# An mLSTM and S5 block: head beginnings, entry of the last head and merge in another order

## The chip, the cores and the metric

The kernel runs on one core of a Trainium2 chip. The metric is the device time of one execution in microseconds (us); lower is better. A core has TensorE (PE, matmuls), VectorE (DVE), ScalarE (ACT), GpSimd (POOL), each with a queue of instructions of its own that it works off in order, and SyncE (SP), whose queue here issues all DMA transfers between DRAM and the on-chip memory. Engines wait for each other through semaphores.

## The reference, cut to what matters

A decoder block over a sequence of 1024 tokens, 1024 channels wide, in float32. Everything is computed from xn, the normalised input:

```python
proj = xn @ w_in[l]
u_a, z_a, o_a, i_a, f_a, u_b, z_b, g_pre = jnp.split(proj, split_points, axis=-1)
y_a = mlstm_branch(u_a, z_a, o_a, i_a, f_a, conv_w[l], conv_b[l], w_q[l], w_k[l], w_v[l],
                   b_i[l], b_f[l], head_g[l], skip_a[l]) @ w_a_out[l]
y_b = s5_branch(...) @ w_b_out[l]
g = jax.nn.sigmoid(g_pre.astype(jnp.float32)).astype(h.dtype)
merged = g[..., :D_MODEL] * y_a + g[..., D_MODEL:] * y_b
h = h + rmsnorm(merged @ w_o[l], norm_post_g[l])
```

The mLSTM branch: c = silu(causal convolution of u_a over 4 tokens), q and k from c, v from u_a, in 4 heads of 256 channels; per head a chunkwise linear attention over 8 chunks of 128 tokens with a running 256 x 256 state; the result times sigmoid(o), normalised per head, times head_g, plus skip times c, times silu(z_a). The S5 branch is done before the stretch that this document is about.

## The kernel before, in words

Every operand of a matmul is split into a high and a low part (suffixes h and l, as xh and xl, wh and wl), and every product is three matmuls: high by high, low by high, high by low, lines 180 to 182. The high part is written by ScalarE (`Copy` into a rounded type), the low part by VectorE or GpSimd (value minus high part). Weights come in as wr and become wh (line 140) and wl (line 142); `take` and `pump` split the next weights ahead of their use.

The order of all instructions is that of the code; nothing reorders them. Work that is not attention is cut into units: a projection of one block of 128 or 256 columns, 24 matmuls of 256 columns or 512 (18 for a y_a unit, which leaves out two of the eight k). They stand in a deque, `fillers`; `fill()` runs the next one, and so the code of a head puts units between the steps of its attention. `run` also does three things around a unit: `tick` issues the stores that wait in `pending`, the loads of the next units are issued (`look` of them ahead), and `step2` runs operations that an earlier unit put off with `defer`.

A head h has for each chunk c: `attn_a(h, c)` (scores of q and k, line 1084, transposes of k, line 1096, and the splits sTh/sTl, ksh/ksl and q2h/q2l by ScalarE and VectorE) and `attn_b(h, c)` (the state and the output, three matmuls each on those splits; VectorE then makes hr). attn_a runs one chunk ahead of attn_b. After chunks 3 and 7 `attn_c` scales hr (line 1170), `attn_d(h, hf)` transposes it (line 1180), adds skip times c and multiplies by silu(z) (lines 1182 and 439), and `attn_e` splits the result and stores it to yh_d and yl_d in DRAM. For the last head the split goes straight into the tiles of k = 6 and 7.

During head h the fillers are the o, u and z units of head h + 1 and `k1`, the second half of k of head h itself. `late` are five units of the next head, run after the last chunk: us[2], ks[0], vs[0], us[3], vs[1] (u for tokens 512 on, two blocks of 128 channels; k and v). A u unit puts off `u_act` and `u_out` (the convolution's silu, its split into hlh and hll, lines 970 to 981, and the store of skip times c to cs_d, line 983). k_unit ends with line 1057, where GpSimd makes q for a half of the sequence, in a single buffer.

In the last head the fillers are the y_a units, (i, half, m): the projection by w_a_out, k = 0 to 5 only. Its input comes back from yh_d and yl_d into the tiles xh and xl, k by k and half by half (`ystep(n)` issues n of these pairs). Each unit loads y_t and y_gb (t1_d and gb_d: gate and S5 part), computes (1 + y_t) times its sum plus a quarter of y_gb (lines 1237, 1238), and stores that to pa_d.

After the heads comes the merge: the last four y_a units (i = 3) are mixed with 16 `mg_unit`s, which add k = 6 and 7 to a block of y_a (weights ya3, their own 2 x 1024 columns), load the stored part (fpa) and the gate (ft), and split the sum into mh and ml. `wo_unit(i, t)`, 32 of them, are the output projection; the fourth of a token block ends with `finish`.

Two pools of PSUM banks hold the sums: `pp` with three banks (units) and `pm` with five (attention).

Of the kernel before, what the change touches and what calls it, by code (L numbers as in the profile page):

```python
# [21 lines left out]
H = 4  # L22
# [14 lines left out]
def hybrid_block(ctx, tc, x, norm_pre_g, w_in, conv_w, conv_b, w_q, w_k, w_v, b_i, b_f, head_g,  # L37
# [1179 lines left out]

    yaux = {}

    def ya_pre(ct, hf, pool=None):  # L1220
        rs = slice(ct * P, (ct + 1) * P)
        pool, a, b, n = (hp, "hlh", "hll", 5) if pool is None else (pool, "ft", "fpa", 7)
        t1 = pool.tile([P, 512], F32, tag=a, bufs=n, name="y_t1")
        SY.dma_start(t1, t1_d[rs, HS[hf]])
        gb = pool.tile([P, 512], F32, tag=b, bufs=n, name="y_gb")
        SY.dma_start(gb, gb_d[rs, HS[hf]])
        yaux[ct, hf] = (t1, gb)

    def ya_unit(i, m, hf):
        if m == 0 and hf == 0 and i < 3:  # L1230
            cur["ya"] = take(("ya", i), i > 0)
        ct = 2 * i + m
        rs = slice(ct * P, (ct + 1) * P)
        t1, gb = yaux.pop((ct, hf))
        o = bank()
        proj_cm(o, cur["ya"], m * P, yh, yl, HS[hf], ks=list(range(6)))
        V.scalar_tensor_tensor(t1, t1, 1.0, o, op0=ALU.add, op1=ALU.mult)
        V.scalar_tensor_tensor(gb, gb, 0.25, t1, op0=ALU.mult, op1=ALU.add)
        store(pa_d[rs, HS[hf]], gb)
# [29 lines left out]
    for h in range(H):  # L1269
# [19 lines left out]
        if h == H - 1:  # L1289
            for i in range(2):  # L1290
                fillers[i][0]()
                fillers[i] = (None,) + fillers[i][1:]
        ystep(4)
        if h < H - 1:
            fill()
        attn_a(h, 0)
        for c in range(NCH):
            if c == 1 or c == 6:
                load_cz(h, c // 4)
            if c == 6 and h == H - 2:  # L1300
# [33 lines left out]
    flush2()
# [6 lines left out]
    mh, ml = {}, {}  # L1341
    maux = {}

    def mg_pre(ct, hf):
        rs = slice(ct * P, (ct + 1) * P)
        t1 = fp.tile([P, 512], F32, tag="ft", bufs=7, name="ft")
        SY.dma_start(t1, t1_d[rs, HS[hf]])
        pr = fp.tile([P, 512], F32, tag="fpa", bufs=7, name="fpa")
        SY.dma_start(pr, pa_d[rs, HS[hf]])
        maux[ct, hf] = (t1, pr)  # L1350

    def mg_unit(ct, hf):
        if ct == 0 and hf == 0:
# [11 lines left out]
    ob, xres = {}, {}  # L1365
    sso = fp.tile([P, NCH, 4], F32, name="sso")

    def wo_unit(i, t):
# [13 lines left out]
        jk = fp.tile([P, 256], F32, tag="fjk", bufs=2, name="fjk")  # L1382
        A.activation(jk, o[:, :256], AF.Square, accum_out=sso[:, t, i:i + 1])
# [15 lines left out]
    def mgf(ct, hf):  # L1399
        fillers.append(unit(lambda: mg_unit(ct, hf), lambda: mg_pre(ct, hf)))  # L1400
# [56 lines left out]
```

## Time and profile before

| what | value |
|---|---|
| median of 3 runs | 1003.8 us (1002.75, 1003.8, 1004.91) |
| profiled execution | 1006.37 us, of which the span in the profile is 1004.3 us |
| TensorE busy | 976.7 us |
| VectorE, ScalarE, GpSimd busy | 615.5, 351.1, 154.6 us |
| mean granted TensorE clock | 0.993 of full speed |

The profile is of one execution. Times in it are microseconds from the span's start; a matmul's end is modelled, since matmuls overlap in the pipe. In a timeline a bracket at a row's end tells how long the engine was idle before it and which instruction (engine, tile, line) ended that; rows of one kind that follow each other are joined (x2). SPq is SyncE's queue.

### The profile page before, as it was taken

To read this page: it belongs to the slowest core of one execution; us is meant where nothing else is said; L and a number is where in the kernel's file an instruction comes from. 1 tells how busy PE (TensorE), PEld (TensorE's weight loads), DVE (VectorE), ACT (ScalarE), POOL (GpSimd) and SP (SyncE) were. 2 spreads that over 40 slices of the span, in tenths; PEclk is the share of its full clock that TensorE was granted. 3 is DMA by queue.
4 is the path that set the end of the run, shared out by engine and by line. 5 is a ranking of instruction groups with operands and counts; after the bars stand their busy time and mean duration, and the time that the engine had idled before them with its cause. 6 is when DMAs were issued, how large, how long until landed. Compare 5 with 4: busy or idle time off the path is not lost.

```text
span 1004.3 us, 15220 instructions
## 1 busy us (share of the span) xinstructions
PE 976.7 (97%) x5617; PEld 840.9 (84%) x5617; DVE 615.5 (61%) x1400; ACT 351.1 (35%) x696; POOL 154.6 (15%) x210
## 2 busy tenths in 40 slices
PE   7999999999999999999999999999999999999997
PEld 6888888788778788978988899889987888779997
DVE  4426496686952854254677477747774888675226
ACT  7322131233032531223544355435543452223311
POOL 4001000000000000012112232223221311343001
PEclk8999999999999999999999999999999999999999
DMA  7344221333056447314433354336436796783504
GB/s 253 94 153 157 90 95 36 93 111 109 17 177 187 170 156 253 107 42 126 138 121 131 95 174 131 135 86 184 132 121 215 248 318 202 271 301 118 189 1 168
DMA packets 115449, 148.31 MB, mean 148 GB/s; under 512 B 19080, under 2 KB 71472, under 8 KB 115376
## 3 DMA queue, kind: packets, MB, share of 16 engines
q1 hardware_dynamic: 115376, 147.35, 45.7%
q8 instruction: 44, 0.72, 0.3%
q14 instruction: 29, 0.24, 0.1%
HBM read 100.88 MB, written 46.43 MB: 147 GB/s over the span
## 4 chain that ended last, share of the span: by engine, by line
PE 83%; DVE 10%; DMA 3%; issue 2%; ACT 1%; SPq 0%; POOL 0%; DVEq 0%; POOLq 0%; ACTq 0%
PE pp L180 22%; PE pp L182 22%; PE pp L181 22%; PE pm L182 4%; PE pm L180 4%; PE pm L181 3%; DVE wl L142 1%; PE pm L1084 1%; DMA wr<-in_w_in_dram 1%; DVE zt L439 1%; PE pm L1007 1%; DMA xt<-in_x_dram 1%; DMA ft<-t_d 1%; PE pm L661 1%; DVE ec_r L439 1%
## 5 line engine op out<-in xcount | busy, mean ns | idle before, releaser
L180 PE MATMUL pp<-xh,wh 128*128 128x512 f32 x768 | 307.6, 401 | 3.2 <-DVE xl L276 2.4
L182 PE MATMUL pp<-xh,wl 128*128 128x512 f32 x768 | 305.0, 397 | 4.4 <-DVE wl L142 4.4
L181 PE MATMUL pp<-xl,wh 128*128 128x512 f32 x768 | 304.7, 397 | 0.0
L182 PEld LDWEIGHTS pp<-xh,wl 128*128 128x128 f32 x768 | 145.0, 189 | 41.0 <-DVE wl L142 6.2
L180 PEld LDWEIGHTS pp<-xh,wh 128*128 128x128 f32 x768 | 145.0, 189 | 39.3 <-DVE xl L276 2.7
L181 PEld LDWEIGHTS pp<-xl,wh 128*128 128x128 f32 x768 | 145.1, 189 | 32.7
L142 DVE TENSOR_TENSOR wl<-wr,wh 128x1024 fp32r<-128x1024 f32 (+2 forms) x71 | 83.4, 1211 | 46.3 <-ACT wh L140 41.7
L140 ACT ACTIVATE wh<-wr 128x1024 fp32r<-128x1024 f32 (+2 forms) x76 | 73.2, 1008 | 40.8 <-PE pm L181 30.7
L182 PE MATMUL pp<-wh,ml 128*128 128x256 f32 x256 | 72.8, 284 | 0.5 <-POOL ml L1363 0.5
L180 PE MATMUL pp<-wh,mh 128*128 128x256 f32 x256 | 72.9, 285 | 0.0
L180 PE MATMUL pp<-wh,xh 128*128 128x256 f32 (+1 forms) x256 | 72.0, 281 | 0.0
L181 PE MATMUL pp<-wl,mh 128*128 128x256 f32 x256 | 71.9, 281 | 0.0
L288 ACT ACTIVATE tg<-pp 128x512 f32<-128x512 f32 x32 | 19.1, 599 | 151.1 <-PE pp L182 75.2
L181 PE MATMUL pp<-wl,xh 128*128 128x256 f32 (+1 forms) x256 | 71.8, 280 | 0.0
L182 PE MATMUL pp<-wh,xl 128*128 128x256 f32 (+1 forms) x256 | 71.8, 280 | 0.0
L182 PEld LDWEIGHTS pp<-wh,ml 128*128 128x128 f32 x256 | 48.1, 188 | 0.7 <-POOL ml L1363 0.7
L181 PEld LDWEIGHTS pp<-wl,mh 128*128 128x128 f32 x256 | 48.6, 190 | 0.1
L180 PEld LDWEIGHTS pp<-wh,mh 128*128 128x128 f32 x256 | 48.4, 189 | 0.2 <-ACT mh L1362 0.2
L181 PEld LDWEIGHTS pp<-wl,xh 128*128 128x128 f32 x256 | 48.2, 188 | 0.2
L180 PEld LDWEIGHTS pp<-wh,xh 128*128 128x128 f32 x256 | 48.1, 188 | 0.2
L182 PEld LDWEIGHTS pp<-wh,xl 128*128 128x128 f32 x256 | 48.0, 187 | 0.0
L981 POOL TENSOR_TENSOR hll<-t2k,hlh 128x512 fp32r<-128x512 f32 x16 | 20.8, 1297 | 166.2 <-ACT hlh L980 89.4
(395 smaller groups left out, 1731.5 us busy)
## 6 DMA issues: line engine op xcount, KB each, us to landing
wr<-in_w_in_dram SPq DMA_DIRECT2D x48, 512.0 KB
t_d<-tg SPq DMA_DIRECT2D x32, 256.0 KB
xt<-in_x_dram SPq DMA_DIRECT2D x8, 512.0 KB
aux<-t_d SPq DMA_DIRECT2D x16, 256.0 KB
gb_d<-aux SPq DMA_DIRECT2D x16, 256.0 KB
so_d<-sow SPq DMA_DIRECT2D x32, 128.0 KB
sz_d<-t2k SPq DMA_DIRECT2D x16, 256.0 KB
cs_d<-t2k SPq DMA_DIRECT2D x16, 256.0 KB
```

What stands on the lines that cost most here:

```text
L140: A.activation(hi, raw, AF.Copy)
L142: eng.tensor_tensor(wl[:, k0:k0 + n, c0:c0 + w], raw, hi.bitcast(F32), op=ALU.subtract)
L180: PE.matmul(o, lh, rh, start=first, stop=False)
L181: PE.matmul(o, lh, rl, start=False, stop=False)
L182: PE.matmul(o, ll, rh, start=False, stop=last)
L288: A.activation(t, o, AF.Tanh, scale=0.5)
L439: V.tensor_tensor(o, a, b, op=op)
L661: PE.matmul(o[NS * b2:NS * (b2 + 1), g * P:(g + 1) * P], q["wt"][:, ri, g, NS * b2:NS * (b2 + 1)], ut[b][:, 2 * g + b2, :], start=True, st ...
L981: PL.tensor_tensor(lo, acc, hi.bitcast(F32), op=ALU.subtract)
L1007: PE.matmul(pm[:, 256 * k:256 * k + 256], wt[:, e, 256 + P * k:256 + P * k + P], wt[:, e, 0:256], start=e == 0, stop=e == 1)
L1084: PE.matmul(sc[:, :P], k_[:, m, sl], q_[:, m, sl], start=m == 0, stop=m == 1)
```

## The change

Five things change. One: at the beginning of each head two fillers run before attn_a(1) and attn_b(0), where one did; one filler fewer follows. Two: at the entry of the last head attn_d(2, 1) comes after us[3], not before it; what is put off is flushed (`flush2`, `tick`) before the head starts; `ystep(2)` issues two pairs of loads there, not four; and in the last head the fillers stand in other places, so that the first y_a unit of the second half (the third unit of the head) runs behind attn_b(0), and k1 before attn_a(3). Three: in the merge the last four y_a units leave their sum in the PSUM bank, and the mg units of the same blocks add k = 6 and 7 to it; these come first in each half; the second half of the weights ya3 is split by GpSimd. Four: wo units are mixed with two fillers each, not three. Five: at the end the sum of three of the four squares is made early, and GpSimd adds the fourth.

```diff
@@ ya_unit
-        proj_cm(o, cur["ya"], m * P, yh, yl, HS[hf], ks=list(range(6)))
+        proj_cm(o, cur["ya"], m * P, yh, yl, HS[hf], ks=list(range(6)), last=i < 3)
+        if i == 3:
+            maux[ct, hf] = (t1, gb, o)
+            return
@@ heads
-        ystep(4)
+        ystep(4 if h < H - 1 else 2)
...
-            fill()
+            fill(2 if c == 0 else 1)
             ystep(3)
...
-            if c % 4 != 3 if h < H - 1 else c in (2, 4, 6):
+            if c in ((1, 2, 4, 5, 6) if h < H - 1 else (4, 6)):
                 fill()
...
-            if i == (3 if h < H - 2 else 2):
+            if i == 3:
                 attn_d(h, 1)
...
+        if h == H - 2:
+            flush2()
+            tick()
...
-    cur["ya"] = take(("ya", 3))
+    cur["ya"] = take(("ya", 3), False)
+    pump(pl=True)
@@ mg_unit
-        t1, pr = maux.pop((ct, hf))
-        o = bank()
-        proj_cm(o, cur["ya3"], ct * P, yh, yl, HS[hf], ks=[6, 7])
+        t1, pr, o = maux.pop((ct, hf))
+        part = o
+        o = bank() if part is None else part
+        proj_cm(o, cur["ya3"], ct * P, yh, yl, HS[hf], ks=[6, 7], first=part is None)
         V.scalar_tensor_tensor(t1, t1, 1.0, o, op0=ALU.add, op1=ALU.mult)
-        tt(t1, t1, pr, ALU.add)
+        if part is None:
+            tt(t1, t1, pr, ALU.add)
+        else:
+            V.scalar_tensor_tensor(t1, pr, 0.25, t1, op0=ALU.mult, op1=ALU.add)
@@ wo_unit
+        if i == 2:
+            V.tensor_reduce(sso[:, t, 4:5], sso[:, t, 0:3], axis=mybir.AxisListType.X, op=ALU.add)
+            V.tensor_scalar(sso[:, t, 4:5], sso[:, t, 4:5], 4.0 * EPS, None, op0=ALU.add)
         if i == 3:
             s = fp.tile([P, 1], F32, tag="fs", bufs=4, name="fs")
-            V.tensor_reduce(s, sso[:, t, :], axis=mybir.AxisListType.X, op=ALU.add)
-            V.tensor_scalar(s, s, 1.0 / D, 4.0 * EPS, op0=ALU.mult, op1=ALU.add)
+            PL.tensor_tensor(s, sso[:, t, 3:4], sso[:, t, 4:5], op=ALU.add)
@@ merge
-    todo = deque((ct, hf) for hf in range(2) for ct in range(KT))
-    for m, hf in ((0, 0), (1, 0), (0, 1), (1, 1)):
-        yaf(m, hf)
-        mgf(*todo.popleft())
-        mgf(*todo.popleft())
-    for ct, hf in todo:
+    yaf(0, 0)
+    yaf(1, 0)
+    for ct in (6, 7, 0, 1, 2, 3):
+        mgf(ct, 0)
+    yaf(0, 1)
+    yaf(1, 1)
+    n_ya = len(fillers)
+    for ct, hf in ((6, 1), (7, 1), (4, 0), (5, 0), (0, 1), (1, 1)):
         mgf(ct, hf)
+    n_hf = len(fillers) - n_ya
+    for ct in range(2, 6):
+        mgf(ct, 1)
...
-        fill(3)
-        if t == 1:
+        fill(2)
+        if t == 2:
             pump()
```

What it moves. First SyncE's queue at the entry of the last head. xh_98 to xh_101 and xl_106 to xl_109 are k = 2 to 5 of the second half, read back; y_t and y_gb belong to a y_a unit. Before, from the last store of head 2:

```order
L82 DMA yl_d<-t2k 128x512
L1066 DMA so<-so_d 128x256 x2
L1224 DMA y_t_7735<-t_d 128x512
L1226 DMA y_gb<-gb_d 128x512
L1215 DMA xh_98<-yh_d 128x512
L1216 DMA xl_106<-yl_d 128x512
L1215 DMA xh_99<-yh_d 128x512
L1216 DMA xl_107<-yl_d 128x512
L1215 DMA xh_100<-yh_d 128x512
L1216 DMA xl_108<-yl_d 128x512
L1215 DMA xh_101<-yh_d 128x512
L1216 DMA xl_109<-yl_d 128x512
```

And in the changed kernel, from the row behind that same store on (xh_101 and xl_109 follow):

```order
L82 DMA cs_d<-t2k 128x512
L1066 DMA so<-so_d 128x256 x2
L1224 DMA y_t_7744<-t_d 128x512
L1226 DMA y_gb<-gb_d 128x512
L1215 DMA xh_98<-yh_d 128x512
L1216 DMA xl_106<-yl_d 128x512
L1215 DMA xh_99<-yh_d 128x512
L1216 DMA xl_107<-yl_d 128x512
L1224 DMA y_t_7768<-t_d 128x512
L1226 DMA y_gb<-gb_d 128x512
L82 DMA pa_d<-y_gb 128x512
L1215 DMA xh_100<-yh_d 128x512
```

The cs_d store has come ahead of all these loads (it stood 20 rows further on), and another y_t, y_gb and a pa_d store ahead of the last four.

Second VectorE in the last head, where the second k unit brings the split of the next weights (L142); sT and q are the products of the next attn_a. Before:

```order
L439 TENSOR_TENSOR ctl<-ct,cth 128x516
L439 TENSOR_TENSOR dec<-dec,msk 128x512
L1237 SCALAR_TENSOR_TENSOR y_t_7763<-y_t_7763,pp 128x512
L1238 SCALAR_TENSOR_TENSOR y_gb<-y_gb,y_t_7763 128x512
L439 TENSOR_TENSOR sT<-pm,dec 128x128
L439 TENSOR_TENSOR q_7970<-q,int 128x256
```

And in the changed kernel, from the same row on:

```order
L439 TENSOR_TENSOR ctl<-ct,cth 128x516
L439 TENSOR_TENSOR dec<-dec,msk 128x512
L142 TENSOR_TENSOR wl<-wr,wh 128x1024
L142 TENSOR_TENSOR wl<-wr,wh 128x512
L439 TENSOR_TENSOR sT<-pm,dec 128x128
L439 TENSOR_TENSOR q_8001<-q,int 128x256
```

The split of the weights stood behind these products and now stands ahead of them; both rows are in the chunk of attn_a(3).

Third VectorE where the merge begins, behind attn_d of the last head. ft and y_t become the merged value, 8598 and 8602 are blocks 6 and 7. Before:

```order
L142 TENSOR_TENSOR wl<-wr,wh 128x1024 x2
L1237 SCALAR_TENSOR_TENSOR y_t_8598<-y_t_8598,pp 128x512
L1238 SCALAR_TENSOR_TENSOR y_gb<-y_gb,y_t_8598 128x512
L1358 SCALAR_TENSOR_TENSOR ft<-ft,pp 128x512
L439 TENSOR_TENSOR ft<-ft,fpa 128x512
```

And in the changed kernel:

```order
L142 TENSOR_TENSOR wl<-wr,wh 128x1024
L1365 SCALAR_TENSOR_TENSOR y_t_8598<-y_t_8598,pp 128x512
L1369 SCALAR_TENSOR_TENSOR y_t_8598<-y_gb,y_t_8598 128x512
L1365 SCALAR_TENSOR_TENSOR y_t_8602<-y_t_8602,pp 128x512
L1369 SCALAR_TENSOR_TENSOR y_t_8602<-y_gb,y_t_8602 128x512
```

One of the two pieces of the split has gone from VectorE (to GpSimd), and blocks 6 and 7 are finished first, without a stored part.

## Rows read from the trace of the kernel before

**Rows 1.** The page, part 1: busy us (share of the span) xinstructions of each engine
```profile
PE 976.7 (97%) x5617; PEld 840.9 (84%) x5617; DVE 615.5 (61%) x1400; ACT 351.1 (35%) x696; POOL 154.6 (15%) x210
```

**Rows 2.** Timeline of TensorE (PE): head beginnings; start, us, line, [idle before <-releaser]
```profile
485.14 0.36 PE L180 MATMUL pm<-vh,ksh 128*128 128x258 f32 x1 [0.66 <-issue]
...
587.67 0.39 PE L180 MATMUL pm<-vh,ksh 128*128 128x258 f32 x1 [0.74 <-ACT ksh L1098]
...
588.50 0.39 PE L182 MATMUL pm<-vh,ksl 128*128 128x258 f32 x1 [0.32 <-DVE ksl L1103]
```

**Rows 3.** Timeline of TensorE: entry of the last head
```profile
777.62 1.46 PE L1180 MATMUL pm<-ident,hr 128*128 128x128 f32 x8 [1.47 <-DVE hr L1170]
...
785.43 0.39 PE L180 MATMUL pm<-wh,hlh 128*128 128x256 f32 x1 [0.40 <-ACT hlh L948]
...
786.16 0.38 PE L182 MATMUL pm<-wh,hll 128*128 128x256 f32 x1 [0.22 <-DVE hll L439]
...
788.50 0.61 PE L1084 MATMUL pm<-q,k 128*128 128x128 f32 x4
...
799.30 0.60 PE L1084 MATMUL pm<-q,k 128*128 128x128 f32 x4
...
801.76 0.40 PE L180 MATMUL pp<-xh,wh 128*128 128x512 f32 x1
...
805.95 0.60 PE L1084 MATMUL pm<-q,k 128*128 128x128 f32 x4
```

**Rows 4.** Timeline of TensorE: the merge
```profile
867.26 0.50 PE L182 MATMUL pp<-xh,wl 128*128 128x512 f32 x1 [0.99 <-DVE wl L142]
...
869.49 0.50 PE L182 MATMUL pp<-xh,wl 128*128 128x512 f32 x1 [1.27 <-DVE wl L142]
...
898.90 0.39 PE L182 MATMUL pp<-wh,ml 128*128 128x256 f32 x1 [0.49 <-POOL ml L1363]
...
902.87 0.50 PE L180 MATMUL pp<-xh,wh 128*128 128x512 f32 x1 [0.56 <-DVE ob L439]
```

**Rows 5.** Timeline of SyncE (SPq): DMA issues at the entry of the last head
```profile
792.78 1.37 SPq L1066 DMA_DIRECT2D so<-so_d  x2
...
799.58 0.46 SPq L1216 DMA_DIRECT2D xl<-yl_d  x1
...
805.37 0.32 SPq L1066 DMA_DIRECT2D so<-so_d  x1
```

**Rows 6.** Timeline of VectorE (DVE): entry of the last head
```profile
785.41 0.69 DVE L439 TENSOR_TENSOR hll<-pp,hlh 128x512 fp32r<-128x512 f32 x1 [1.25 <-ACT hlh L948]
...
795.13 0.69 DVE L971 SCALAR_TENSOR_TENSOR t2k<-t2k 128x512 f32<-128x512 f32 x1
...
811.94 0.42 DVE L1149 SCALAR_TENSOR_TENSOR hr<-so,pm 128x256 f32<-128x256 f32 x1 [0.76 <-DMA so<-so_d]
...
813.36 1.83 DVE L142 TENSOR_TENSOR wl<-wr,wh 128x1024 fp32r<-128x1024 f32 x2 [0.40 <-ACT wh L140]
```

**Rows 7.** Timeline of GpSimd (POOL): entry of the last head, and the end
```profile
798.90 1.29 POOL L981 TENSOR_TENSOR hll<-t2k,hlh 128x512 fp32r<-128x512 f32 x1 [7.54 <-ACT hlh L980]
...
800.16 0.71 POOL L983 TENSOR_SCALAR t2k<-t2k,par 128x512 f32<-128x512 f32 x1
...
808.24 2.78 POOL L1057 TENSOR_TENSOR q<-hlh,hll 128x512 f32<-128x512 f32 x2 [7.38 <-DVE q L439]
...
999.39 0.54 POOL L1389 TENSOR_TENSOR fs<-fs,halfm 128x1 f32<-128x1 f32 x1 [2.34 <-DVE fs L1388]
```

**Rows 8.** Timeline of ScalarE (ACT): second key unit of the last head, and the end
```profile
812.27 1.58 ACT L140 ACTIVATE wh<-wr 128x1024 fp32r<-128x1024 f32 x2
...
998.06 0.38 ACT L1383 ACTIVATE fjk<-pp 128x256 f32<-128x256 f32 x1 [2.40 <-PE pp L182]
```

**Rows 9.** Windows: busy time of each engine, granted TensorE clock, DMA share, GB/s
```profile
300.00:305.00 5.00, 4.27 (x22) 4.11 (x22) 2.52 (x4) 0.00 (x0) 0.00 (x0) 0.66 0.28 106
...
796.00:806.00 10.00, 10.00 (x55) 8.48 (x54) 9.11 (x25) 4.79 (x13) 1.97 (x2) 1.00 0.97 334
```

More of the change, by code (lines that the diff above doesn't have):

```diff
@@ L1216, in ystep @@
             SY.dma_start(yl[k][:, HS[hf]].bitcast(F32), yl_d[k * P:(k + 1) * P, HS[hf]])
-    yaux = {}
+    yaux, maux = {}, {}
     def ya_pre(ct, hf, pool=None):
         rs = slice(ct * P, (ct + 1) * P)
-        pool, a, b, n = (hp, "hlh", "hll", 5) if pool is None else (pool, "ft", "fpa", 7)
+        pool, a, b, n = (hp, "hlh", "hll", 5) if pool is None else (pool, "fyt", "fyg", 2)
         t1 = pool.tile([P, 512], F32, tag=a, bufs=n, name="y_t1")
@@ L1341, in hybrid_block @@
     mh, ml = {}, {}
-    maux = {}
     def mg_pre(ct, hf):
         rs = slice(ct * P, (ct + 1) * P)
-        t1 = fp.tile([P, 512], F32, tag="ft", bufs=7, name="ft")
+        t1 = fp.tile([P, 512], F32, tag="ft", bufs=6, name="ft")
         SY.dma_start(t1, t1_d[rs, HS[hf]])
-        pr = fp.tile([P, 512], F32, tag="fpa", bufs=7, name="fpa")
+        pr = fp.tile([P, 512], F32, tag="fpa", bufs=4, name="fpa")
         SY.dma_start(pr, pa_d[rs, HS[hf]])
-        maux[ct, hf] = (t1, pr)
+        maux[ct, hf] = (t1, pr, None)
     def mg_unit(ct, hf):
-        if ct == 0 and hf == 0:
+        if "ya3" not in cur:
             cur["ya3"] = take("ya3", False)
-        t1, pr = maux.pop((ct, hf))
-        o = bank()
-        proj_cm(o, cur["ya3"], ct * P, yh, yl, HS[hf], ks=[6, 7])
+        t1, pr, o = maux.pop((ct, hf))
+        part = o
+        o = bank() if part is None else part
+        proj_cm(o, cur["ya3"], ct * P, yh, yl, HS[hf], ks=[6, 7], first=part is None)
         V.scalar_tensor_tensor(t1, t1, 1.0, o, op0=ALU.add, op1=ALU.mult)
-        tt(t1, t1, pr, ALU.add)
+        if part is None:
+            tt(t1, t1, pr, ALU.add)
+        else:
+            V.scalar_tensor_tensor(t1, pr, 0.25, t1, op0=ALU.mult, op1=ALU.add)
         mh[ct, hf] = fp.tile([P, 512], F32R, name=f"mh{ct}{hf}")
@@ L1365, in hybrid_block @@
     ob, xres = {}, {}
-    sso = fp.tile([P, NCH, 4], F32, name="sso")
+    sso = fp.tile([P, NCH, 5], F32, name="sso")
     def wo_unit(i, t):
@@ L1382, in wo_unit @@
         jk = fp.tile([P, 256], F32, tag="fjk", bufs=2, name="fjk")
-        A.activation(jk, o[:, :256], AF.Square, accum_out=sso[:, t, i:i + 1])
+        A.activation(jk, o[:, :256], AF.Square, scale=1.0 / 32.0, accum_out=sso[:, t, i:i + 1])
         mul(ob[t][:, cs], o[:, :256], gpo[:, cs])
+        if i == 2:
+            V.tensor_reduce(sso[:, t, 4:5], sso[:, t, 0:3], axis=mybir.AxisListType.X, op=ALU.add)
+            V.tensor_scalar(sso[:, t, 4:5], sso[:, t, 4:5], 4.0 * EPS, None, op0=ALU.add)
         if i == 3:
             s = fp.tile([P, 1], F32, tag="fs", bufs=4, name="fs")
-            V.tensor_reduce(s, sso[:, t, :], axis=mybir.AxisListType.X, op=ALU.add)
-            V.tensor_scalar(s, s, 1.0 / D, 4.0 * EPS, op0=ALU.mult, op1=ALU.add)
+            PL.tensor_tensor(s, sso[:, t, 3:4], sso[:, t, 4:5], op=ALU.add)
             PL.tensor_tensor(s, s, halfm[:, 0:1], op=ALU.pow)
@@ L1399, in mgf @@
     def mgf(ct, hf):
-        fillers.append(unit(lambda: mg_unit(ct, hf), lambda: mg_pre(ct, hf)))
+        fillers.append(unit(lambda: mg_unit(ct, hf), lambda: (ct, hf) in maux or ct > 5 or mg_pre(ct, hf)))
     def yaf(m, hf):
         fillers.append(unit(lambda: ya_unit(3, m, hf), lambda: ya_pre(6 + m, hf, fp)))
-    todo = deque((ct, hf) for hf in range(2) for ct in range(KT))
-    for m, hf in ((0, 0), (1, 0), (0, 1), (1, 1)):
-        yaf(m, hf)
-        mgf(*todo.popleft())
-        mgf(*todo.popleft())
-    for ct, hf in todo:
+    yaf(0, 0)
[6 more added lines that the diff above has]
+    for ct, hf in ((6, 1), (7, 1), (4, 0), (5, 0), (0, 1), (1, 1)):
         mgf(ct, hf)
+    n_hf = len(fillers) - n_ya
+    for ct in range(2, 6):
+        mgf(ct, 1)
     look[0] = 3
@@ L1415, in hybrid_block @@
         fillers[i] = (None,) + fillers[i][1:]
-    fill(10)
+    fill(n_ya)
     pump()
-    fill(4)
+    fill(n_hf)
     for t in range(NCH):
         run(unit(lambda: wo_unit(0, t)))
-        fill(3)
-        if t == 1:
+        fill(2)
+        if t == 2:
             pump()
```

## The prediction

> **What bounds the kernel now.** First the page's busy times: TensorE works 97% of the span [rows 1], so the kernel is bound by its matmuls, and only what TensorE loses by waiting can be gained without taking matmuls away. The change takes none away. Second, therefore, the timeline of TensorE at the places that the diff touches, read by the brackets: idle time before a matmul, and who released it. They show three groups of waits. At the beginning of heads 0, 1 and 2 attn_b(0) waits for the splits of attn_a [rows 2]: 0.66 us in head 0, 0.74 and 0.32 in head 1, and the same pair once more in head 2, so 2.78 us in five waits. At the entry of the last head it waits 1.47 us for hr and 0.40 and 0.22 us for the split u of the last v unit, 2.09 us in three waits [rows 3]. In the merge it waits 0.99 and 1.27 us for the low part of the last y_a weights, 0.49 for ml and 0.56 for a bank that VectorE's ob still holds, 3.31 us in four waits [rows 4]. A wait costs somewhat more than its bracket, since the pipe fills again: the matmul after one shows 0.50 us [rows 4] where an undisturbed one of that shape shows 0.40 [rows 3], and the next starts late as well. I charge 0.15 us for each. Third, the queue of SyncE, because the last head reads its operands back from DRAM while TensorE uses them, and all DMAs stand in that one queue: loads are issued 0.6 us apart there [rows 5], and the 16 DMA engines are 97% busy at 334 GB/s from 796 to 806 us, while TensorE is busy without a gap [rows 9]. That cover is complete, but with nothing to spare.
>
> **The change part by part.**
>
> Head beginnings. With two projection units ahead of attn_a(1), two of 24 short matmuls lie between attn_a(0) and attn_b(0) where one lay, nearly 3 us more in which ScalarE and VectorE make sTh, ksh and ksl. What was missing is under 1.4 us a head, so all five waits are covered: 2.78 + 5 x 0.15 = 3.5 us. Against it stands the tanh of the added o unit, which now stands in ScalarE's queue ahead of attn_a(1)'s operations and writes one of two sow buffers, whose stores were issued late. I leave 0.5 us for that in all three heads (no row shows such a wait; between 0 and 1.5, since the matmuls behind it need these operations only one unit later). Term: -3.0 (-3.5 to -2.0).
>
> Entry of the last head, what goes. attn_d(2,1) comes after the unit us3, 24 long matmuls later, so hr is long scaled when its transposes come; and the transposes stand between us3 and the v unit, which gives the split of u another 1.2 us. 2.09 + 3 x 0.15 = 2.5 us, of which I leave 0.1. Term: -2.4.
>
> Entry of the last head, what comes. The deferred operations of us3 are now flushed before the head starts. They end in a store of c·skip (cs_d) by SyncE, and this store stands ahead of so, of y_t and y_gb and of the loads xh, xl 2 to 5 of the second half; before, it stood behind all of them. With ystep(2) in place of 4, a further pair y_t, y_gb and a pa_d store are also ahead of the last four loads. At the same time the first y_a unit that reads this second half comes earlier: it ran after attn_b(1), and now after attn_b(0).
>
> When can the store be issued? It needs GpSimd's L983, behind L981, behind ScalarE's hlh and VectorE's L971. Before, L971 came 9.7 us after the unit's hll, from 785.41 to 795.13 [rows 6], and the operations between are as long in the new order (four of attn_d, some 2.8 us, take the place of sT, ksl and one y_t, y_gb pair). The unit's hll itself comes 1.62 us of wait and some 1.2 us of transposes (1.46 in their row, with the pipe's end) earlier, at 782.6. So L971 ends at 782.6 + 9.7 + 0.7 = 793.0, hlh 0.6 later, L981 takes 1.29 and L983 0.71 [rows 7]: the store issues at 795.6 in the clock of the old trace. SyncE then needs for the twelve loads what it needed from 792.78 to 799.58, 6.8 us [rows 5], and for the store and three more entries 4 x 0.65: the last xl is issued at 805.0, where it was issued at 799.58.
>
> When has it landed? In bytes, 15 times 256 KB (the two so count as one), 3.93 MB, stand from the store to that load; at 334 GB/s [rows 9] they take 11.8 us, to 807.4, with no delay at either end. From the other side, the so load issued at 805.37 [rows 5] released VectorE at 811.94 [rows 6], 6.6 us later in a full queue: 805.0 + 6.6 = 811.6. I take the middle, 809.5.
>
> When is it wanted? attn_a(0) starts at 788.50 less 2.4, at 786.1. From there to attn_a(2) TensorE took 10.8 us and for attn_a(2) with attn_b(1) 2.46 us, and the unit 4.2 us [rows 3]. The unit now follows after the same 10.8, from 796.9 to 801.1. With the last load at 809.5 and two matmuls behind it, it ends at 810.0. Term: +8.9 (+6.4 to +11.0; less if the DMA engines move these loads faster than the row's mean).
>
> The k unit. It runs before attn_a(3), where it ran after it, and it carries the split of the next y_a weights with it: VectorE's wl, 1.83 us, which waits for ScalarE's wh, 1.58 us [rows 6, 8], stands ahead of the products sT and q2 of attn_a(3). The two GpSimd operations that make q for the second half wait for that q2 (one buffer) and take 2.78 us [rows 7]. From the end Z of the delayed unit: VectorE, busy with its backlog, is through dec at about Z + 6.2; ScalarE's exponentials, k copies and wh, then wl, end at Z + 11.3; q2 at Z + 11.9; q at Z + 14.6. TensorE reaches attn_a(4) after two pairs of attn_a and attn_b (2 x 2.46), the k unit (2.5) and one y_a unit (4.2): Z + 11.9 with attn_a's part of it. Term: +2.4 (+1.0, if VectorE catches up during the long wait, to +3.9).
>
> The clock. The window from 300 to 305 has a mean granted clock of 0.66 [rows 9], a mix of the two levels 2.4 and 1.2 GHz, with TensorE idle for 0.73 us of it: 0.34 of 5 us, 1.7 us lost. An idle time of 9 us should bring at least one such fall. Term: +1.7 (0 to +3.4, a fall of twice the length). The Trainium skill, TensorE: Matmul & The Clock Gate, section "HAM oscillation — how this bites in real kernels", says that an engine left waiting on DMA is throttled again and begins its next work at half clock; by that rule the term belongs in the sum, and without it the sum would be 1.7 less. The low clock of that window agrees with it.
>
> The merge. The order ya, ya, mg of the same blocks puts 8.4 us of matmuls between the unit's start and the first use of the last weights, where 4.2 lay; the wait was 2.3 us, so it is covered, whichever of the two engines makes the second half. ml and ob get a unit more of cover by two fillers between wo units instead of three. The partial sum stays in its bank, so 12 DMAs and 8 VectorE operations go; the queue is not full there, and they free nothing that TensorE waits for. What may be late next is the pair of loads y_t, y_gb of the second half, and I see a slack of one unit for it. 3.31 + 4 x 0.15 = 3.9, and a smaller wait between them: term -4.0 (-4.4 to -2.5).
>
> The end. After the last matmul, ScalarE's square at 998.06 [rows 8] is followed by VectorE's ob, reduce and scalar, and GpSimd's power at 999.39 [rows 7]. Now GpSimd adds the accumulated column itself, right behind the square: the power starts about 0.45 earlier. Term: -0.45 (-0.6 to 0, an added GpSimd operation may take as long as the two that go).
>
> **The sum.** Gains -3.0 - 2.4 - 4.0 - 0.45 = -9.85; costs 8.9 + 2.4 + 1.7 = 13.0; together +3.15. The profiled execution took 1006.37 us, a span of 1004.3 with 2.07 around it; the median of the runs is 1003.8, 0.26% below. The difference is carried over as it stands: 1003.8 + 3.15 = 1007.0.
>
> **Rivals.** First, faster: the queue catches up. After the store nothing else is wanted from the DMA engines, the loads land at the low bound, the clock stays up, and the second wait is only 1.0: -9.85 + 6.4 + 1.0 = -2.45, 1001.4; if they move faster than the mean row, 1000 or less. For it: only four stores stand ahead of this store, so the DMA engines have little else to do, while the mean of rows 9 was under steady load. Against it: 6.6 us from issue to landing. It decides from three costs that together stay under 7.8 us. The Trainium skill, DMA: Bandwidth & Descriptors, "Where 436 GB/s comes from", puts the limit of one core's HBM traffic at about 358 GB/s; by that the bytes would take 11.0 us, 0.8 less than by the row. Chance 0.18.
>
> Second, even: the loads land at 808, the clock does not fall: -9.85 + 7.4 + 2.4 = 0, 1003.8. Chance 0.18.
>
> Third, worse: landing at the upper bound, a long stretch at 1.2 GHz and 3.0 at q: -9.85 + 11.0 + 3.4 + 3.0 = +7.5, 1011.3. Chance 0.13.
>
> Fourth, the change doesn't do what it says: the merge keeps a wait under another name (GpSimd's half of the weights or ml), the heads one on the sow store; half the gain there goes, 3.5 more than the forecast: 1010.5. Chance 0.06.
>
> **How the numbers follow.** The forecast, 1007.0, has 0.45; its own range is 1004.5 to 1009.5. For 8 in 10 the range takes in most of the first and the third rival: 1000.5 to 1011.3. Measurements of this kernel tell 0.2%, 2.0 us, from no change, so faster means under 1001.8 and slower over 1005.8. Faster: most of the first rival and a little of the second, 0.19. Same: the rest of these two and the low edge of the forecast, 0.21. Slower: 0.60.
>
> **What would show it.** In the changed profile: waits at ksh and ksl of the first three heads, at hr, at wl and at ob gone; at the entry of the last head, behind the first attn_b, TensorE idle for some 9 us on matmuls with xh and xl, released by their DMAs; the cs_d store in SyncE's queue released by GpSimd's t2k, with the loads behind it; an idle time of 1 to 4 us at attn_a(4), released by GpSimd's q; the granted clock under 1 just behind the first of these. I am wrong if the loads of the second half are issued before the cs_d store or land by 803, or if the wait at q2 doesn't show.

## The result, and the profile after

The changed kernel takes 1010.88 us (median of 4 runs, 1010.0 to 1013.86) where the kernel before took 1003.27 in the same session (4 runs, 1001.88 to 1004.91): a ratio of 1.0073, 95% interval 1.005 to 1.0096. By the ratio it is slower by 7.3 us (5 to 9.6). The prediction was +3.15 us, 1007.0, in a range from 1000.5 to 1011.3: the side and, in the main, the mechanism were right, and the size was less than half of what came.

The two profiled executions can't be subtracted as wholes: the first attn_a of head 0 stands at 480.17 us in the kernel before and at 477.80 in the changed one, though nothing ahead of it differs. So the time is compared in five stretches, each from one matmul to another that both kernels have, and each with the kernel before as the base:

| stretch of TensorE | before, us | changed kernel |
|---|---|---|
| A: first attn_a of head 0 to last attn_a of head 2 | 267.48 | -1.8 |
| B: from there to the first attn_a of head 3 | 40.85 | -2.9 |
| C: from there to its last attn_a | 51.96 | +13.7 |
| D: last transposes of attn_d to the last matmul | 137.11 | -1.6 |
| E: last matmul to the span's end | 6.62 | -0.3 |

Between C and D lie 20.1 us that are the same in both. The sum is +7.1 us, which is what the runs show (7.3).

First the new waits of TensorE behind the heads, from the list for the changed kernel: what it waited for, us in total, how often, the longest.

```profile
PE pp L180 <- DMA xh<-yh_d: 6.2, 2, 4.4
...
PE pp L180 <- DVE ft L1365: 2.1, 1, 2.1
...
PE pm L1084 <- POOL q L1057: 0.9, 1, 0.9
PE pp L182 <- POOL ml L1373: 0.9, 1, 0.9
```

The waits of [rows 2], [rows 3] and those on wl and ob of [rows 4] are all gone, as intended; the one on ml is longer. Two more new waits come in heads 1 and 2, at the second filler and at attn_b(1). TensorE's timeline in head 1:

```profile
583.08 0.39 PE L180 MATMUL pp<-wh,xh 128*128 128x256 f32 x1 [0.32 <-ACT sow L835]
...
592.52 0.36 PE L180 MATMUL pm<-vh,sTh 128*128 128x258 f32 x1 [0.20 <-DVE hr L1149]
```

The entry of the last head on the same engine. The rows of L1084 are attn_a(0), (2) and (3), which stand in [rows 3] at 788.50, 799.30 and 805.95:

```profile
781.38 0.60 PE L1084 MATMUL pm<-q,k 128*128 128x128 f32 x4
...
798.45 0.80 PE L180 MATMUL pp<-xh,wh 128*128 128x512 f32 x1 [4.38 <-DMA xh<-yh_d]
...
803.92 0.80 PE L180 MATMUL pp<-xh,wh 128*128 128x512 f32 x1 [1.78 <-DMA xh<-yh_d]
...
806.97 1.05 PE L1084 MATMUL pm<-q,k 128*128 128x128 f32 x4
...
813.83 0.60 PE L1084 MATMUL pm<-q,k 128*128 128x128 f32 x4
```

The third y_a unit begins in time and stops in its k = 2 and again in k = 4. SyncE's queue tells why, to be held against [rows 5]: the last yl store, the cs_d store, then xh of k = 2 and xh of k = 4.

```profile
788.42 0.32 SPq L82 DMA_DIRECT2D yl_d<-t2k  x1
...
791.70 0.32 SPq L82 DMA_DIRECT2D cs_d<-t2k  x1
...
793.99 0.42 SPq L1215 DMA_DIRECT2D xh<-yh_d  x1
...
797.56 0.67 SPq L1215 DMA_DIRECT2D xh<-yh_d  x1
```

The entries behind the store follow with gaps of at most 0.5 us, and the store comes 3.3 us after the entry ahead of it. What it waited for stands in GpSimd's timeline:

```profile
789.68 1.29 POOL L981 TENSOR_TENSOR hll<-t2k,hlh 128x512 fp32r<-128x512 f32 x1 [1.29 <-ACT hlh L980]
```

and the chain of waits, followed back from the last instruction, names the way from there (start, us, what):

```profile
790.97 0.72 POOL t2k L983
791.70 0.32 SPq L82
...
793.09 3.24 DMA y_t<-t_d
796.42 0.70 DVE y_t L1240
797.15 0.37 SPq L82
797.56 6.32 DMA xh<-yh_d
...
819.26 2.75 POOL q L1057 x2
```

ScalarE's hlh, then GpSimd's L981 and L983, then the store, as the prediction had it. From the store to the load of k = 4 the chain goes by the load of y_t behind the store, VectorE's L1240 and the pa_d store; SyncE's own row has hardly a gap there and, as far as its pace tells, would have come to that store at the same time, so that no single one of these sets the load's issue. The load of k = 4 then takes 6.3 us from issue to the matmul that needs it. Last, the granted clock in windows of 5 us (the third number from the right):

```profile
795.00:800.00 5.00, 1.44 (x3) 0.79 (x3) 3.36 (x10) 1.90 (x6) 0.00 (x0) 0.68 0.96 317
...
800.00:805.00 5.00, 3.22 (x7) 1.50 (x6) 1.03 (x3) 0.85 (x3) 0.00 (x0) 0.50 1.03 371
...
805.00:810.00 5.00, 5.00 (x20) 4.23 (x20) 2.65 (x7) 0.98 (x3) 0.00 (x0) 0.50 1.05 394
...
810.00:815.00 5.00, 5.00 (x31) 4.46 (x31) 3.24 (x10) 2.23 (x6) 0.00 (x0) 0.95 0.52 144
```

While TensorE idles the clock falls to 0.50, that is 1.2 GHz, and it stays there until about 810.5, some 12 us after the first load has come; a matmul behind a wait lasts 0.80 us in it, where one at the full clock lasts 0.50 [rows 4]. From 800 to 810 the DMA engines move 371 and 394 GB/s, more than both rates that the prediction reckoned with.

### The profile page after: what moved, and what is told of

Same layout as the page of the kernel before. It is cut to its first block, busy times and chain, and to the rows that moved or that the text cites. A ratio compares the mean times of both kernels' runs of the same rounds, so it can differ in the third digit from the quotient of the medians.

```text
span 1009.0 us, 15188 instructions
## 1 busy us (share of the span) xinstructions
PE 978.4 (97%) x5617; PEld 841.1 (83%) x5617; DVE 611.3 (61%) x1391; ACT 351.6 (35%) x696; POOL 160.1 (16%) x219
## 4 chain that ended last, share of the span: by engine, by line
PE 80%; DVE 9%; DMA 4%; issue 3%; POOL 3%; ACT 1%; SPq 1%; DVEq 0%; POOLq 0%; ACTq 0%
PE pp L180 21%; PE pp L182 21%; PE pp L181 21%; PE pm L180 3%; PE pm L182 3%; PE pm L181 3%; PE pm L1084 1%; POOL t2k L1200 1%; DVE wl L142 1%; DMA wr<-in_w_in_dram 1%; DVE zt L439 1%; PE pm L1007 1%; POOL wl L142 1%; DMA xt<-in_x_dram 1%; DMA xh<-yh_d 1%
## 5 line engine op out<-in xcount | busy, mean ns | idle before, releaser
L142 DVE TENSOR_TENSOR wl<-wr,wh 128x1024 fp32r<-128x1024 f32 (+2 forms) x70 | 80.6, 1186 | 52.4 <-ACT wh L140 47.9
L981 POOL TENSOR_TENSOR hll<-t2k,hlh 128x512 fp32r<-128x512 f32 x16 | 20.7, 1295 | 158.7 <-ACT hlh L980 81.8
```

The costliest lines, as they stand in the source:

```text
L142: eng.tensor_tensor(wl[:, k0:k0 + n, c0:c0 + w], raw, hi.bitcast(F32), op=ALU.subtract)
L981: PL.tensor_tensor(lo, acc, hi.bitcast(F32), op=ALU.subtract)
```

## The experiments

Each ran beside the kernel before on the same chip. Two numbers are given: the ratio of the runs to the kernel before with its 95% interval, which has about 0.2% of noise to each side, and the change of the five stretches of the profiled execution against the kernel before. Where the code is the same, E repeats to 0.1 us, A to 0.6 and C to 1.2 (+2.1, +2.4, +2.6 and +3.3 in the four kernels whose last head differs from before by attn_d's place alone); D, and B in one case, vary more, of which the section on the hardware tells. Of D a single trace tells little: the five kernels with the old merge take 135.7 to 138.3 us there.

**The last head undone.** Changed kernel, with

```diff
-        if h == H - 2:
-            flush2()
-            tick()
...
-        ystep(4 if h < H - 1 else 2)
+        ystep(4)
...
-            fill(2 if c == 0 else 1)
+            fill(2 if c == 0 and h < H - 1 else 1)
...
-            if c in ((1, 2, 4, 5, 6) if h < H - 1 else (4, 6)):
+            if c in ((1, 2, 4, 5, 6) if h < H - 1 else (2, 4, 6)):
```

> The changed kernel with the last head as before in three points: no flush ahead of it, ystep(4), and the fillers in their old places (third y_a unit behind attn_b(1), k1 behind attn_a(3)); attn_d after us[3], the head beginnings, the merge and the end stay changed. Theory (the loss of 13.8 us between the first and the fifth attn_a of the last head comes from these three edits alone): the rest of the change keeps its gains, 1.8 in the heads, 2.9 at attn_d, 1.5 in the merge, 0.3 at the end, so 1003.3 - 6.5 = 996.8 us, with no idle time on xh or xl in TensorE's row. Rival (attn_d's new place is itself late for the last head, by taking VectorE from the splits or SyncE from the loads): a wait of several us stays there, and 1000 us or more.

Measured: 0.9964 (0.9945 to 0.9984); A -1.5, B -2.9, C +3.3, D -2.1, E -0.3, together -3.6. The three edits do make most of the loss, 10.4 of 13.7 us, but 3.3 us stay, so the rival has a part. Most of them are waits at the first attn_b, in TensorE's timeline (another 0.61 and 0.17 us are waits on xh and xl in the third y_a unit, at 803.4 and 804.1):

```profile
783.92 0.61 PE L1084 MATMUL pm<-q,k 128*128 128x128 f32 x4
...
790.68 0.39 PE L180 MATMUL pm<-vh,ksh 128*128 128x258 f32 x1 [1.08 <-ACT ksh L1098]
...
791.50 0.39 PE L182 MATMUL pm<-vh,ksl 128*128 128x258 f32 x1 [0.31 <-DVE ksl L1103]
```

And VectorE in the same kernel, the first of attn_d's operations and the sT behind them:

```profile
785.68 0.74 DVE L1182 SCALAR_TENSOR_TENSOR t2k<-pm,par,cz 128x512 f32<-128x512 f32 x1
...
789.64 0.28 DVE L439 TENSOR_TENSOR sT<-pm,dec 128x128 f32<-128x128 f32 x1
790.30 0.75 DVE L439 TENSOR_TENSOR sTl<-sT,sTh 128x128 fp32r<-128x128 f32 x1 [0.38 <-ACT sTh L1092]
```

The same operations in the kernel before:

```profile
781.31 0.74 DVE L1182 SCALAR_TENSOR_TENSOR t2k<-pm,par,cz 128x512 f32<-128x512 f32 x1
...
792.39 0.28 DVE L439 TENSOR_TENSOR sT<-pm,dec 128x128 f32<-128x128 f32 x1
793.04 0.29 DVE L439 TENSOR_TENSOR sTl<-sT,sTh 128x128 fp32r<-128x128 f32 x1 [0.38 <-ACT sTh L1092]
```

sT comes 5.7 us after attn_a(0) (783.92); before it was 3.9 (792.39 after 788.50). TensorE comes 2.9 us earlier to the last head, VectorE only 1.1: the four operations of attn_d stood ahead of the convolution, in a time in which VectorE else waits for ScalarE (hll in [rows 6]), and now stand behind it. And sTl takes 0.75 us in place of 0.29, since it waits for GpSimd, of which the section on the hardware tells.

**attn_d alone.** Kernel before, with

```diff
-            if i == (3 if h < H - 2 else 2):
+            if i == 3:
```

> The kernel before with attn_d(2, 1) behind us[3] and nothing else. Theory (the wait is moved, not removed): the waits on hr, hlh and hll go, 2.9 us earlier at the last head's first attn_a, but attn_d's four VectorE operations now stand behind the convolution of us[3] and ahead of sT, so attn_b(0) waits 1.1 us on ksh and 0.3 on ksl and the loads of the second half, for which nothing is earlier, are waited for as well: a net of -0.5 to +0.5, ratio 0.9995 to 1.0005. Rival (the step of the prediction): -2.4 us stay, ratio 0.9976.

Measured: 0.9985 (0.9965 to 1.0004); B -2.9, C +2.1, D +1.2, of which C shows the same two waits, 1.08 and 0.31 us. Of the 2.9 us 0.9 remain in this trace, as the expectation's theory had it. By the four kernels with attn_d in that place, C costs 2.1 to 3.3, so that the move gains 0.9 us at best and loses 0.4 at worst: neither the runs nor the stretches tell that from nothing.

**The queue alone.** Kernel before, with

```diff
-        ystep(4)
+        ystep(4 if h < H - 1 else 2)
...
+        if h == H - 2:
+            flush2()
+            tick()
```

> The kernel before with the flush ahead of the last head and ystep(2) alone; the third y_a unit stays behind attn_b(1). Theory (two things have to meet: loads that are issued late and a unit that comes early): the loads land some 4 us later than before, while the unit had next to no slack, so a wait of 2 to 4 us on xh, no fall of the clock, 1003.3 + 3 = 1006 us. Rival one (the place of the unit alone is the cause): 1003.3, no wait. Rival two (the queue's order alone is the cause): a wait of 6 us and more, a fall of the clock, 1011 us.

**The fillers alone.** Kernel before, with

```diff
-            fill()
+            fill(2 if c == 0 and h == H - 1 else 1)
...
-            if c % 4 != 3 if h < H - 1 else c in (2, 4, 6):
+            if c % 4 != 3 if h < H - 1 else c in (4, 6):
```

> The kernel before with the last head's fillers in their new places alone (third y_a unit behind attn_b(0), k1 ahead of attn_a(3)); the queue keeps its order. Theory (both have to meet): the unit comes 2.5 us earlier than before and finds its last loads not landed: a wait of 2 to 3 us, and 1.5 to 2.5 us at q in attn_a(4), 1003.3 + 4.5 = 1008 us. Rival one (the place of the unit alone): a wait of 6 us and more, 1013 us. Rival two (the queue alone): only the wait at q, 1005 us.

Measured: queue alone 1.004 (1.0022 to 1.0058), C +4.1; fillers alone 1.0052 (1.0031 to 1.0074), C +5.8, A and B unchanged in both but for a fall of the clock in B of the first (+1.6). Either costs by itself, at two places each, so the theory that both have to meet is refuted. The queue, in TensorE's timeline:

```profile
795.33 0.39 PE L182 MATMUL pm<-vh,ksl 128*128 128x258 f32 x1 [0.82 <-DVE ksl L1103]
...
807.12 0.49 PE L180 MATMUL pp<-xh,wh 128*128 128x512 f32 x1 [1.24 <-DMA xh<-yh_d]
```

The second row is the load, late by the store, and by the y_t, y_gb pair that ystep(2) puts ahead of it; no run tells these two apart. The first is the flush. Of its operations VectorE's L971 stands ahead of sT, ScalarE's hlh ahead of sTh, and GpSimd's L981 holds up VectorE's sTl, 1.26 us in place of 0.29:

```profile
793.62 1.26 DVE L439 TENSOR_TENSOR sTl<-sT,sTh 128x128 fp32r<-128x128 f32 x1 [0.70 <-ACT sTh L1092]
```

```profile
793.46 1.27 POOL L981 TENSOR_TENSOR hll<-t2k,hlh 128x512 fp32r<-128x512 f32 x1 [2.44 <-ACT hlh L980]
```

The fillers:

```profile
805.96 0.50 PE L181 MATMUL pp<-xl,wh 128*128 128x512 f32 x1 [0.57 <-DMA xl<-yl_d]
...
822.57 0.49 PE L1084 MATMUL pm<-q,k 128*128 128x128 f32 x2 [1.31 <-POOL q L1057]
...
823.99 0.49 PE L1084 MATMUL pm<-q,k 128*128 128x128 f32 x2 [0.92 <-POOL q L1057]
```

Here the loads are issued as before and the unit comes to them too early (3.0 us lost over its 18 matmuls, from the times of its rows), and q is late, 2.7 us.

**One of the two undone.** The two halves of the first experiment's diff, each by itself: changed kernel with the last head's fillers as before (its last four lines), and changed kernel without the flush and with ystep(4) (its first five).

> The changed kernel with the last head's fillers in their old places; flush, queue and ystep(2) stay changed. Theory (the costs in the last head add up: attn_d's place 2.1 to 3.3 us, queue 4.1, fillers 5.8): from the first to the last attn_a 6.5 to 7.5 us more than before, ratio 1.0005 to 1.001. Rival (they hide each other, since one wait covers the other): 4 us, ratio 0.9975. Second rival (the late unit finds everything landed): 3 us, ratio 0.9965.

> The changed kernel without the flush and with ystep(4); the last head's fillers stay in their new places. Theory (the costs add up): attn_d's place 2.1 to 3.3 us and fillers 5.8, 8 to 9 us more than before from the first to the last attn_a, ratio 1.0015 to 1.0025, no fall of the clock. Rival (the early unit alone makes most of the loss): 11 us or more with a fall of the clock, ratio 1.005 or more.

Measured: fillers undone 1.0009 (0.9992 to 1.0026), C +7.4; queue undone 1.0009 (0.9995 to 1.0023), C +9.3. With the last head undone at +3.3 this gives a square: +3.3 with neither, +7.4 with the queue, +9.3 with the fillers, +13.7 with both. Added up, 3.3 + 4.1 + 6.0 = 13.4. Neither edit needs the other to do harm, and the costs add. That they add so well is in part luck, for the clock is in three of the four: it fell in the kernel with the queue, from 790.5 to 797.5, and twice in the one with the fillers, 797.4 to 800.8 and 817.9 to 821.3, where the forecast was no fall; in the kernels with one edit alone, 4.1 and 5.8, it didn't fall in this stretch. Windows of the first, then of the second kernel:

```profile
790.00:795.00 5.00, 3.89 (x13) 3.31 (x14) 4.73 (x11) 2.09 (x8) 1.90 (x2) 0.56 0.42 133
```

```profile
795.00:800.00 5.00, 3.41 (x8) 1.76 (x9) 3.86 (x12) 2.75 (x8) 0.00 (x0) 0.74 1.00 352
...
815.00:825.00 10.00, 8.90 (x43) 7.74 (x44) 9.46 (x24) 4.81 (x11) 2.11 (x4) 0.83 0.59 193
```

With the old fillers the flush shows as a wait of attn_b(0), TensorE's timeline of that kernel:

```profile
790.46 0.47 PE L180 MATMUL pm<-vh,ksh 128*128 128x258 f32 x1 [3.13 <-ACT ksh L1098]
```

With both edits this wait isn't there, since two units lie ahead of attn_b(0); the time comes back as a wait for loads.

**The store alone.** Changed kernel, with the cs_d store held back behind the loads of the second half:

```diff
             flush2()
+            cs_store = pending.pop()
             tick()
...
+            if c == 1 and h == H - 1:
+                pending.append(cs_store)
```

> The changed kernel with the flush where it is, but the cs_d store held back and put into SyncE's queue behind the loads of the second half (after the first chunk). Theory (the loads are late because that store waits for GpSimd at the head of the queue, 3.3 us from the yl store before it to its own issue): the loads are issued some 3 us earlier, TensorE idles 3 us less on xh, the clock falls for a shorter time or not at all: from the first to the last attn_a 8 to 10 us more than before in place of 13.7, ratio 1.002 to 1.004 to the kernel before. Rival (the other operations of the flush, or the DMA engines' rate, set the landing): 12 us or more, ratio 1.006 to 1.008.

Measured: 1.0059 (1.0038 to 1.0079); C +10.8, so 2.9 us come back, about as much as the loads are issued earlier (xh of k = 4 stands 13.0 us behind attn_a(0), where it was 16.2), and the rest doesn't. That is between the two forecasts: by the stretch a little nearer to the theory, by the ratio at the edge of the rival. SyncE issues xh of k = 4 at 801.05, and the matmul that waits for it is

```profile
808.06 0.80 PE L180 MATMUL pp<-xh,wh 128*128 128x512 f32 x1 [1.78 <-DMA xh<-yh_d]
```

7.0 us from issue to use. The loads themselves are slow there, with the DMA engines at 0.96 to 1.05 of their time in all windows of 5 us from 800 to 815; and the pair y_t, y_gb and the pa_d store are still ahead of the last four.

**The heads alone.** Kernel before, with

```diff
-            fill()
+            fill(2 if c == 0 and h < H - 1 else 1)
...
-            if c % 4 != 3 if h < H - 1 else c in (2, 4, 6):
+            if c in ((1, 2, 4, 5, 6) if h < H - 1 else (2, 4, 6)):
```

> The kernel before with the changed beginnings of heads 0, 1 and 2 alone. Theory (what the changed kernel's trace shows): 1.1 us gained in head 0 and 0.3 to 0.4 each in heads 1 and 2, where new waits on sow (0.3) and hr (0.2) take the rest: -1.8 us, ratio 0.998. Rival (the step of the prediction): -3.0, ratio 0.997, with no wait over 0.1 us in those heads.

Measured: 0.9973 (0.9951 to 0.9995); A -1.6, and the two waits on sow and hr as in the changed kernel. The stretch says 1.4 to 2.0 in every kernel with this edit; the interval of the runs holds the prediction's 3.0 too.

**The merge.** Changed kernel, with the load of the output weights four units later:

```diff
     fill(n_ya)
     pump()
-    fill(n_hf)
+    late_fetch = pending.pop()
+    fill(4)
+    pending.append(late_fetch)
+    fill(n_hf - 4)
```

> The changed kernel with one line moved in the merge: the loads of the next output weights (wr from w_o) are put into the queue four units later, so that the ft and fpa loads of those units stand ahead of them. Theory (the wait of 2.1 us on ft and the 0.9 us on ml behind it come from ft loads that stood behind those weight loads, which waited 10 us for a free buffer): both waits go, 1010.9 - 3 = 1008 us. Rival (the loads are late because the DMA engines are slow there, or the weights are then late): the wait moves to wl or stays, 1010.5 to 1011.5 us.

Measured: 1.0049 (1.0029 to 1.007), that is 0.24% less than the changed kernel's ratio, though the two intervals overlap; D -3.0 in place of -1.6. The wait on ft is gone. That on ml, which was to go too, stays and is longer, 0.26 and 1.05 us in place of 0.86. The second of them in TensorE's timeline:

```profile
905.81 0.38 PE L182 MATMUL pp<-wh,ml 128*128 128x256 f32 x1 [1.05 <-POOL ml L1373]
```

**Put together.** The first experiment's diff and the late load's in one kernel, and the same with attn_d in its old place:

```diff
-            if i == 3:
+            if i == (3 if h < H - 2 else 2):
```

> The changed kernel with the last head's queue, flush and fillers as before (attn_d stays behind us[3]) and with the load of the next output weights put four units later in the merge. Theory: the gains of both add up, 3.6 us from the first and 1.5 to 2.4 from the second: -5.5 us against the kernel before, ratio 0.9945. Rival (the merge's wait on ml takes the place of the one on ft): -3.6 to -4, ratio 0.996.

> The same, with attn_d(2, 1) in its old place too, ahead of us[3]. Theory (attn_d's new place is worth nothing): within 0.5 us of the one with attn_d behind us[3], ratio 0.994 to 0.995. Rival (its gain stays): 2.4 us slower than that one, ratio 0.997.

Measured: 0.9957 (0.9932 to 0.9982) and 0.9957 (0.9936 to 0.9978). Stretches: -5.8 and -4.4 in sum; B and C together are -0.5 with attn_d moved and +0.4 without. This pair, too, gives attn_d's move 0.9 us, less than the 1.2 to which C repeats. The ratio lies nearer to the first one's rival (0.996) than to its theory.

**The merge's order.** The first of these two, with blocks 4 and 5 of the first half ahead of the last two y_a units:

```diff
-    for ct in (6, 7, 0, 1, 2, 3):
+    for ct in (6, 7, 0, 1, 2, 3, 4, 5):
...
-    for ct, hf in ((6, 1), (7, 1), (4, 0), (5, 0), (0, 1), (1, 1)):
+    for ct, hf in ((6, 1), (7, 1), (0, 1), (1, 1)):
```

> The version with the old last head and the late weight load (attn_d behind us[3]), and in the merge the mg units of blocks 4 and 5 of the first half moved ahead of the last two y_a units. Theory (the waits of 0.26 and 1.06 us on ml are left because GpSimd makes ml of blocks 4 and 5, which the first wo unit reads, last of a row of six at 1.6 us each): both go, and nothing comes in their place, from the last transposes to the last matmul 1.4 us less than in that version, ratio to the kernel before 0.994 to 0.995. Rival (eight mg units in a row wait for their loads, four buffers deep): a wait on ft or fpa of 1 us and more, ratio 0.996 or above.

Measured: 996.58 us where the kernel before took 1004.96, ratio 0.9925 (0.99 to 0.9951); A -2.0, B -2.9, C +2.6, D -5.0, E -0.3, together -7.5. No wait of the merge is left; D is 2.0 us less than in the version that this one starts from, where 1.4 was forecast. This version beats both kernels.

## Why the prediction was right in kind and wrong in size

**Entry of the last head: right, 13.0 forecast, 13.7 measured.** The store was forecast at 795.6 of the old trace, in which the last attn_a of head 2 stands 4.2 us later than in the new one; that gives 791.4, and it issued at 791.70. The end of the delayed unit was to cost 8.9 us; to attn_a(2) 10.6 were lost, of which the half pace of its last six matmuls (803.92 to 806.97, 3.05 us where they take 1.4) is 1.6. The clock costs another 1.6 behind it (attn_a(2) to attn_a(3) takes 6.86 us, and 5.25 in the kernel with the fillers alone), so both together 3.2 where the term was 1.7, its bound 3.4. The wait at q was to be 2.4; it cost 1.5, which is luck of a kind. VectorE did not catch up: from the end of the delayed unit (806.97) its dec ends 6.4 us later, forecast 6.2, and q 15.1, forecast 14.6. It was TensorE that came 1.6 us late, at the low clock; with the fillers alone, at the full clock, q costs 2.7. VectorE's row in the changed kernel:

```profile
812.68 0.68 DVE L439 TENSOR_TENSOR dec<-dec,msk 128x512 f32<-128x512 f32 x1
```

So the clock's term was mis-sized, and a part of the excess came back at q. (The window from 300 to 305, from which the term was taken, stands behind waits for VectorE, 1.31 and 0.73 us, not for DMA; the fall behind a wait for loads is first seen here.) Of the loss up to the unit's end the prediction named three causes, the store, the pair of loads behind it and the early unit, and gave them one price; holding back the store alone gives back 2.9 of 13.7, and the early unit costs 3.0 with the queue as before.

**attn_d: the term was -2.4; it measures -2.9 to the first attn_a and +2.1 to +3.3 behind it.** The step that failed is "attn_d(2,1) comes after the unit us3 ... so hr is long scaled": it asked what TensorE waits for and not where VectorE does attn_d's products. This error stayed hidden: in the changed kernel two units lie ahead of attn_b(0), no wait shows there, and the loss of the entry came out right without it. What attn_d's place costs inside the 13.7 us no run shows.

**Heads: -3.0 forecast, -1.8 measured.** Head 0 gave 1.1; in heads 1 and 2 the waits of [rows 2] went, and 0.32 and 0.20 us came, with the refilling 0.5 and 0.4. I had named the tanh of the added unit and left it 0.5 us for all three heads. What waits is not ScalarE for the sow buffer: a unit's first matmul waits for the bank of pp that sow reads, and sow stands on ScalarE behind attn_e's copy, which itself waited for VectorE:

```profile
582.12 0.63 ACT L1196 ACTIVATE t2k<-t2k 128x512 fp32r<-128x512 f32 x1 [0.84 <-DVE t2k L439]
582.66 0.37 ACT L835 ACTIVATE sow<-pp 128x256 f32<-128x256 f32 x1
```

**Merge: -4.0 forecast, -1.6 measured** (-1.6 to -2.6 in the five kernels with this merge, all against the one trace of before). All four waits of [rows 4] went or shrank, and one came that the prediction looked for in the wrong row: not y_t and y_gb of the second half but ft. SyncE's queue there:

```profile
884.83 0.32 SPq L1355 DMA_DIRECT2D fpa<-pa_d  x1
...
895.49 1.52 SPq L124 DMA_DIRECT2D wr<-in_w_o_dram  x2
...
897.06 0.50 SPq L1353 DMA_DIRECT2D ft<-t_d  x1
```

The weight load stood 10.7 us for a buffer that VectorE was still to split (wl from 894.24 on), and the ft loads stood behind it. VectorE's row, and the matmul that waits for it:

```profile
903.03 0.69 DVE L1365 SCALAR_TENSOR_TENSOR ft<-ft,pp 128x512 f32<-128x512 f32 x1 [2.08 <-DMA ft<-t_d]
```

```profile
903.87 0.35 PE L180 MATMUL pp<-wh,mh 128*128 128x256 f32 x1 [2.12 <-DVE ft L1365]
```

It is the mechanism of the last head once more, a blocked entry at the head of one queue. The late load took 1.5 us of it away by this pair of traces, and 0.7 by the mean of the three kernels with it against that of the five without; the order of blocks took another 2.0, in one trace.

**The end: -0.45 forecast, -0.3 measured.** GpSimd's addition takes 0.19 us, and the power starts 1.19 us after the last matmul's start where it was 1.71, 0.5 earlier; why only 0.3 of it arrive at the span's end no run shows:

```profile
1003.86 0.55 POOL L1401 TENSOR_TENSOR fs<-fs,halfm 128x1 f32<-128x1 f32 x1
```

**The sum.** Against the terms the stretches are off by +1.2 us in the heads, -0.5 in B, +0.7 in C, +2.4 in the merge and +0.15 at the end, 3.95 together. Nearly all of it, 3.6, is the gains in the heads and the merge that did not come. That is the prediction's fourth rival, which had 3.5 more than the forecast, 1010.5, and a chance of 0.06: waits under other names, one of them at sow (though not for its store) and one on ml; the largest, on ft, it did not name. So the terms of the entry, on which the working was spent, held, and the gains, which were added up from the brackets that would go, did not; for each wait that goes, the next in line on the engines that feed TensorE was not looked up. That 1010.88 still lies in the range is luck: its upper end came from the third rival, a worse entry, which is not what happened.

## What to carry to other kernels

Where one queue issues all transfers, a store that waits for an engine is a wait for every load behind it (3.3 us at the cs_d store and 10.7 at the weight load here): look at each entry moved ahead of loads for the instant when its data is ready, not for its bytes. A wait taken away on a busy engine is a gain only if the engines that feed it come earlier too; follow their rows to the next meeting point before the gain is counted. And compare stretches between matmuls that both traces have, and more than one trace of the same code, since single executions differ by more than such an edit is worth.

## What the runs showed of the hardware

The same wait lowers TensorE's clock in one execution and not in another. Behind the two waits on wl (0.99 and 1.27 us) the kernel before kept the full clock, and the one with attn_d alone, whose code is the same there, did not:

```profile
866.00:874.00 8.00, 5.74 (x24) 4.17 (x23) 7.30 (x8) 1.14 (x2) 3.47 (x3) 1.00 0.99 350
```

```profile
869.00:877.00 8.00, 6.25 (x20) 4.75 (x21) 6.67 (x8) 0.63 (x1) 2.86 (x2) 0.79 0.80 262
```

0.21 of 8 us, 1.7 us. Of the five kernels with this piece of code two fell, and in one of five the clock fell behind the wait on hr, at the entry. In the same way the waits at q, 1.31 and 0.92 us in the fillers alone and in the kernel with the queue undone, lowered it in the second only, where attn_a(4) to attn_a(5) takes 9.48 us in place of 7.95. That is the noise of B and a part of that of D, which without the two falls still differs by 1.4 us in the five.

And an operation of VectorE can last until GpSimd's is through. sTl, 128x128 in 0.29 us, ends 0.14 to 0.16 us after GpSimd's L981 or L1200 (128x512) whenever it starts while one of these runs: in before, changed kernel, last head undone and queue alone that is 41 of 41, up to 1.30 us, and all others take 0.29, the few beside GpSimd's 128x4 operations (L1162) too. So the flush costs not only by the queue: it brings L981 to where attn_b(0) needs sTl and ksl.
